# Last norm of a transformer-like layer: the scaled and shifted rows summed by TensorE in PSUM

## The chip, the cores and the metric

The kernel runs on one core of a Trainium2 chip. A core has five engines that run on their own and meet at semaphores: TensorE (PE in the profile; PEld is its weight load), VectorE (DVE), ScalarE (ACT), GpSimd (POOL), which has no access to PSUM here, and SyncE (SP), which issues the transfers that sixteen DMA engines carry out. SBUF is the working memory, PSUM the memory in which TensorE sums. The metric is the time of one execution in device microseconds, the median of several runs.

## The reference

One step of one decoder layer for 256 prompt tokens and 8x4 sample tokens, 288 tokens in all, with 2048 features. A combined input projection feeds a short gated convolution and a dilated window attention; both branches are gated, summed and projected. A layer norm follows, then a gated feed-forward net with a convolution, and the last norm:

```python
x1 = LN1(ALPHA * x + mixed @ w_out)
a, b = split(x1 @ w_up); a = causal_conv3(a)
y  = LN2(ALPHA * x1 + (silu(a) * b) @ w_down)
LN(d) = (d - mean(d)) * rsqrt(var(d) + 1e-5) * g + b       # mean and variance over the 2048 features of a token
```

All is float32. The caches are also copied to outputs. The change is in LN2 alone.

## The kernel before

Features lie on the partitions: an activation is 16 blocks of 128 features by 288 tokens. Every weight block (128 outputs by up to 16x128 inputs) is loaded from memory by SP (`prepare`, L181), cut in two parts hi and lo by ScalarE and VectorE (`split`, L230: a cast, then the remainder), in half blocks of eight 128x128 pieces with four buffers for each part, and multiplied in three terms per piece, hi x hi, hi x lo, lo x hi (`mms`, L219; lines 225, 226, 227). A product of a whole block is 48 matmuls of 288 columns, and its sum lies in one of six PSUM buffers `acc`. The same `prepare` sends, behind some loads, a copy from memory to memory of a part of the caches.

The feed-forward net runs in three parts of 16, 16 and 12 feature blocks: up products, convolution and gate, then 16 down products whose results are added to `dd`, the 16 blocks that go into LN2. In the last part each down product has 12x3 matmuls. After each of them VectorE adds the product to `dd` (L913), ScalarE squares it (L755) and GpSimd adds block and square to two sums (L760, L761); from block 1 on GpSimd has taken a rough mean `c` off the block beforehand (L910). The last block joins in TensorE: `ones_d` times the sums and the last block gives mean and mean square of each token on all partitions (L769, L770).

`finish_out` (L795) then forms the output. ScalarE squares and copies the mean (L800, L801), VectorE gets the variance (L802), ScalarE takes the reciprocal square root and its square (L808, L809), and VectorE refines it in one Newton step (L819, L820). r = 1/deviation stands in PSUM, a copy for GpSimd in SBUF (L821). Mean and r are rows by token, so they are taken off and multiplied in wide operations over 2 or 3 blocks (`by_token`, L806), on VectorE for most blocks and on GpSimd for the rest, as the lists at the top of the file say: `NORM_DVE` (L90), `MEAN_POOL`, `OUT_POOL`. The scale g and the shift b are by feature, one number per partition: ScalarE applies them in one activation per block (L830), VectorE does it for four blocks (L828). The result lies in `yah`, and six transfers, in the order of `OUT_ORDER` (L94), bring it out (L831).

The order on each engine is made by a scheduler that plans the whole program with its own estimates; `issue_after` and `behind` pin an instruction behind another. The instructions of one engine run in that order.

Of the kernel before, what the change touches and what calls it, by code (L numbers as in the profile page):

```python
# [14 lines left out]
ALU = mybir.AluOpType  # L15
# [71 lines left out]

NORM_DVE = ("m", 0, 3), ("r", 0, 3), ("m", 3, 3), ("r", 3, 3), ("m", 6, 2), ("r", 6, 2), ("r", 8, 2), ("r", 10, 2)  # L90
MEAN_POOL = (8, 2), (10, 2), (12, 2), (14, 2)
OUT_POOL = (12, 2), (14, 2)
GB_DVE = (8, 9, 10, 11)
OUT_ORDER = (0, 3), (3, 3), (6, 2), (8, 4), (12, 2), (14, 2)  # L94


@with_exitstack
def layer_kernel(ctx: ExitStack, tc: tile.TileContext, ins, outs):
# [14 lines left out]
    def sb(pl, shape, tag, dt=F32, bufs=None):  # L113
        return pl.tile(shape, dt, tag=tag, name=nm(tag), bufs=bufs)
# [10 lines left out]
    def t2(ap):  # L125

        return ap.rearrange("p (a h) -> p h a", h=2)
# [4 lines left out]
    def f32(ap):  # L132
        return ap.bitcast(F32)
# [595 lines left out]

    dd = sb(big, [P, KD, T], "dd")  # L730

    lw = sb(wk, [P, 7, T], "cache", bufs=3)

    class Norm:


        def __init__(self, g, b, tail):

            self.g, self.b, self.tail = g, b, tail
            self.s1, self.s2, self.c = (lw[:, k] for k in range(3))  # L740

        def first(self):

# [7 lines left out]
        def add(self, i):  # L751
            d = dd[:, i]
            last = i == KD - 1
            q = self.s2 if i == 0 else sb(wk, [P, T], "cy", bufs=2)
            act.activation(q, d, AF.Square)  # L755
            i_sum = None
            if i == 0:
                i_sum = pool.tensor_copy(self.s1, d)
            elif not last or not self.tail:
                pool.tensor_tensor(self.s1, self.s1, d, ALU.add)  # L760
                i_sum = pool.tensor_tensor(self.s2, self.s2, q, ALU.add)  # L761
            if i == KD - 2:

                act.activation(lw[:, 3, 0:1], q[:, 0:1], AF.Abs_reciprocal_sqrt)
            if last:
                self.p1, self.p2 = att(T), att(T)
                if self.tail:
                    for p, s, e in ((self.p1, self.s1, d), (self.p2, self.s2, q)):
                        pe.matmul(p, f32(ones_d), s, start=True, stop=False)  # L769
                        pe.matmul(p, f32(ones_d), e, start=False, stop=True)  # L770
                else:
                    w = sb(wk, [P, 4, T], "cache", F32R, bufs=3)
                    split(w[:, 0:2], w[:, 2:4], lw[:, 0:2])
# [6 lines left out]

        def finish(self):

            mu, v, r, t = (lw[:, k] for k in range(3, 7))
# [11 lines left out]
        def finish_out(self, y, out):  # L795

            mu, r_pool, t = (lw[:, k] for k in range(3, 6))
            mean, v = self.p1, self.p2
            r, dev = (sb(ps, [P, T], "acc") for _ in range(2))
            act.activation(t, mean, AF.Square)  # L800
            act.copy(mu, mean)  # L801
            i_v = dve.scalar_tensor_tensor(v, v, EPS, t, ALU.add, ALU.subtract)  # L802

            def by_token(eng, k0, n, w, op):
                k = slice(k0, k0 + n)
                return eng.tensor_tensor(dd[:, k], dd[:, k], w.unsqueeze(1).broadcast_to([P, n, T]), op)  # L806

            act.activation(r, v, AF.Abs_reciprocal_sqrt)  # L808
            act.activation(t, r, AF.Square)  # L809
            for k0, n in MEAN_POOL:  # L810
                by_token(pool, k0, n, mu, ALU.subtract)
            before = i_v
            for n_op, (what, k0, n) in enumerate(NORM_DVE):
                with tc.issue_after(before.ins):
                    before = by_token(dve, k0, n, *((mean, ALU.subtract) if what == "m" else (dev, ALU.mult)))
                if n_op == 0:

                    with tc.issue_after(before.ins):
                        dve.scalar_tensor_tensor(t, t, -0.5, v, ALU.mult, ALU.mult)  # L819
                        before = dve.scalar_tensor_tensor(dev, t, 1.5, r, ALU.add, ALU.mult)  # L820
                    act.copy(r_pool, dev)  # L821
            for k0, n in OUT_POOL:
                by_token(pool, k0, n, r_pool, ALU.mult)
            for k0, n in OUT_ORDER:
                for i in range(k0, k0 + n):
                    if i in GB_DVE:
                        with tc.issue_after(before.ins):
                            dve.tensor_scalar(t2(y[:, i]), h2(dd[:, i]), self.at(self.g, i), self.at(self.b, i), ALU.mult, ALU.add)  # L828
                    else:
                        act.activation(t2(y[:, i]), h2(dd[:, i]), AF.Identity, bias=self.at(self.b, i), scale=self.at(self.g, i))  # L830
                sp.dma_start(out[:, k0 : k0 + n, :], y[:, k0 : k0 + n, :])  # L831

# [31 lines left out]
    cf = sb(big, [P, KF, 2 + 2 * NB], "qk_s")  # L864
    f = 0
    n2 = Norm(R_LN + 2 * KD, R_LN + 3 * KD, True)
    sums = []
    for part, nf in enumerate(THIRDS):
        gh = sb(big, [P, KD, T], "yah", F32R)
        gl = sb(big, [P, KD, T], "yal", F32R)  # L870
        for k in range(nf):
            pa = product(x_gb if part == 0 else x)
            u = sb(wk, [P, UW + 2], "u", bufs=2)
            up, us = conv_in(u[:, :UW], R_SF + f * 2 * NB)
            if part == 0:
                pa, b1 = normed(pa)
                for a, b in zip(of_tokens(up, us), of_halves(pa)):
                    act.activation(a, b, AF.Identity, bias=b1)
            else:
# [12 lines left out]
            f += 1  # L892
            if part == 0:

                with tc.issue_after(i_rows.ins):
                    pool.tensor_tensor(dd[:, k], dd[:, k], n1.r, ALU.mult)
                    pool.tensor_tensor(dd[:, k], dd[:, k], n1.nmr, ALU.add)
                act.activation(dd[:, k], dd[:, k], AF.Identity, bias=n1.at(n1.b, k), scale=n1.at(n1.g, k))
        if f == KF:
            sp.dma_start(outs["o_cf"].rearrange("p (k r) -> p k r", k=KF), cf)  # L900
        for i in range(KD):
            o = product((h3(gh), h3(gl)))
            if part == 0:
                for i_x, *before in zip(split(x[0][:, i], x[1][:, i], h2(dd[:, i])), last_split, w_split):
                    for b in before:
                        behind(i_x, b)
                dve.scalar_tensor_tensor(h2(dd[:, i]), h2(dd[:, i]), ALPHA, o, ALU.mult, ALU.add)
            else:
                if f == KF and i > 0:
                    i_c = pool.tensor_tensor(dd[:, i], dd[:, i], n2.c, ALU.subtract)  # L910
                    if i > 2:
                        behind(i_c, sums[i - 3])
                dve.tensor_tensor(h2(dd[:, i]), h2(dd[:, i]), o, ALU.add)  # L913
            if f == KF:
                if i == 0:
                    n2.first()
                sums.append(n2.add(i))
    yf = sb(big, [P, KD, T], "yah")
    y_out = outs["o_y"].rearrange("p (k t) -> p k t", k=KD)
    n2.finish_out(yf, y_out)  # L920


# [181 lines left out]
```

## Time and profile before

| | |
|---|---|
| median of 3 runs | 1725.01 us (1724.82 to 1725.48) |
| the profiled execution: its own time | 1724.86 us |
| its span, first to last instruction | 1723.1 us |
| TensorE busy | 1704.4 us, 99% |
| VectorE, ScalarE, GpSimd busy | 1107.7, 870.7 and 271.1 us |
| moved by DMA | 436.16 MB, mean 253 GB/s |

A row of a timeline has the start in microseconds, the duration, the engine, the source line, the operation, what it writes `<-` what it reads with the shapes, `xN` for N merged instructions, and in brackets how long the engine was idle ahead of it and what released it. A row of the chain of waits has start, duration and the work that the end waited on. A row of a table by stretches has the stretch, its length, busy time and count of PE, PEld, DVE, ACT and POOL, the granted TensorE clock (1.00 is full), the mean busy share of the DMA engines, and GB/s. In a group of instructions the last numbers are busy microseconds, mean nanoseconds of one, and the idle time ahead of it. The rows for one line have the shortest, the median and the longest duration in nanoseconds.

### The profile page before, as it was taken

The page shows a single profiled execution, that of the slowest core. Times are in us where ns is not written, and L with a number is a line of the kernel's source. Part 1 is how long each engine was busy: PE and PEld are TensorE (multiplying, and loading weights), DVE is VectorE, ACT ScalarE, POOL GpSimd, SP SyncE. Part 2 cuts the span into 40 slices and gives each one's busy share as a digit, 9 for nine tenths or more (in the row PEclk, how much of TensorE's full clock was granted, in tenths as well). Part 3 has the DMA queues.
Part 4 walks back from the last instruction along what each step waited for, and adds up shares of the span by engine and source line. Part 5 has one row for each costly group of instructions (what it writes and reads, how often), then busy time and mean ns, then how long its engine had stood idle before and what let it go on. Part 6 is the DMA issues. An engine that isn't in the chain of part 4 may idle for free.

```text
span 1723.1 us, 33696 instructions
## 1 busy us (share of the span) xinstructions
PE 1704.4 (99%) x14096; PEld 1699.0 (99%) x14096; DVE 1107.7 (64%) x1428; ACT 870.7 (51%) x1416; POOL 271.1 (16%) x428
## 2 busy tenths in 40 slices
PE   9999999999999999999999999999999999999996
PEld 9999999999999999999999999999999999999996
DVE  6457677775777765455788888855555554555554
ACT  5446555554555554444545655544454543354444
POOL 0011110000000000011454333300111100011165
PEclk9999999999999999999999999999999999999998
DMA  8766666665667776688876666667666667767662
GB/s 294 288 258 250 237 220 252 234 242 205 262 245 253 297 285 245 245 308 302 300 264 245 246 258 254 245 251 276 255 253 261 245 250 265 268 249 261 234 233 92
DMA packets 60408, 436.16 MB, mean 253 GB/s; under 512 B 7584, under 2 KB 13472, under 8 KB 20640
## 3 DMA queue, kind: packets, MB, share of 16 engines
q1 hardware_dynamic: 58960, 430.33, 66.9%
q10 hardware_dynamic: 1296, 3.69, 0.6%
q8 instruction: 110, 1.80, 0.4%
q14 instruction: 42, 0.34, 0.1%
HBM read 427.53 MB, written 94.53 MB: 303 GB/s over the span
## 4 chain that ended last, share of the span: by engine, by line
PE 98%; DMA 0%; DVE 0%; ACT 0%; SPq 0%; ACTq 0%; issue 0%; DVEq 0%
PE acc L225 32%; PE acc L226 32%; PE acc L227 32%; PE acc L310 2%; DMA wst<-in_w_in 0%; ACT yah L830 0%; DVE dd L806 0%; PE att L513 0%; PE att L434 0%; PE att L417 0%; PE att L383 0%; PE acc L422 0%; PE att L390 0%; PE att L543 0%; PE att L430 0%; SPq L273 0%
## 5 line engine op out<-in xcount | busy, mean ns | idle before, releaser
L231 DVE TENSOR_TENSOR wlo<-wst,whi 128x1024 fp32r<-128x1024 f32 (+1 forms) x574 | 699.9, 1219 | 482.4 <-ACT whi L231 478.5
L231 ACT CAST whi<-wst 128x1024 fp32r<-128x1024 f32 (+1 forms) x574 | 586.4, 1022 | 777.7 <-PE acc L226 710.8
L225 PE MATMUL acc<-xh,whi 128*128 128x288 f32 (+1 forms) x3184 | 909.3, 286 | 0.0
L226 PE MATMUL acc<-xl,whi 128*128 128x288 f32 (+1 forms) x3184 | 907.7, 285 | 0.0
L227 PE MATMUL acc<-xh,wlo 128*128 128x288 f32 (+1 forms) x3184 | 907.6, 285 | 0.0
L225 PEld LDWEIGHTS acc<-xh,whi 128*128 128x128 f32 x3184 | 599.1, 188 | 1.4 <-issue 0.8
L227 PEld LDWEIGHTS acc<-xh,wlo 128*128 128x128 f32 x3184 | 599.1, 188 | 0.0
L226 PEld LDWEIGHTS acc<-xl,whi 128*128 128x128 f32 x3184 | 599.0, 188 | 0.0
L227 PE MATMUL acc<-yah,wlo 128*128 128x288 f32 x1216 | 347.7, 286 | 0.0
L226 PE MATMUL acc<-yal,whi 128*128 128x288 f32 x1216 | 347.7, 286 | 0.0
L225 PE MATMUL acc<-yah,whi 128*128 128x288 f32 x1216 | 347.6, 286 | 0.0
L227 PEld LDWEIGHTS acc<-yah,wlo 128*128 128x128 f32 x1216 | 229.8, 189 | 0.0
L226 PEld LDWEIGHTS acc<-yal,whi 128*128 128x128 f32 x1216 | 229.8, 189 | 0.0
L225 PEld LDWEIGHTS acc<-yah,whi 128*128 128x128 f32 x1216 | 229.7, 189 | 0.0
L667 POOL COPY qk_s<-u 128x2 f32<-128x2 f32 x44 | 37.9, 861 | 572.0 <-ACT u L881 449.1
L484 DVE TRANSPOSE_TENSOR_REDUCE sw<-cache 128x32 f32<-128x1024 f32 x64 | 79.6, 1244 | 5.2 <-ACT cache L477 1.1
L655 DVE SCALAR_TENSOR_TENSOR cy<-u,prm,cy 128x304 f32<-128x304 f32 x120 | 70.7, 589 | 3.5 <-ACT cy L653 0.7
L726 POOL TENSOR_TENSOR ya<-ya,dd 128x288 f32<-128x288 f32 x16 | 13.7, 859 | 294.4 <-DVE ya L725 288.8
L477 ACT ACTIVATE cache<-cache,qk_s 128x128 f32<-128x128 f32 x128 | 43.2, 392 | 0.0
L477 ACT ACTIVATE cache<-cache,dd 128x128 f32<-128x128 f32 x128 | 42.1, 390 | 0.0
L678 DVE TENSOR_TENSOR ya<-cy,acc 128x256 f32<-128x256 f32 x88 | 23.3, 303 | 28.1 <-PE acc L227 28.1
L231 ACT CAST yah<-ya 128x288 fp32r<-128x288 f32 x76 | 32.5, 427 | 15.7 <-DVE ya L683 8.0
(206 smaller groups left out, 972.2 us busy)
## 6 DMA issues: line engine op xcount, KB each, us to landing
wst<-in_w_in SPq DMA_DIRECT2D x111, 1024.0 KB, 4.9
wst<-in_w_up SPq DMA_DIRECT2D x88, 1024.0 KB, 4.9
wst<-in_w_down SPq DMA_DIRECT2D x32, 1024.0 KB, 4.8
cache<-in_ck SPq DMA_DIRECT2D x18, 1024.0 KB, 6.2
cache<-in_cv SPq DMA_DIRECT2D x18, 1024.0 KB, 6.1
wst<-in_w_a SPq DMA_DIRECT2D x16, 1024.0 KB, 5.0
wst<-in_w_out SPq DMA_DIRECT2D x16, 1024.0 KB, 5.0
wst<-in_w_down SPq DMA_DIRECT2D x16, 768.0 KB, 4.4
```

Of the source, the lines that this page charges most:

```text
L225: pe.matmul(out, hi[:, c, :], xh_k, start=k == 0, stop=False)
L226: pe.matmul(out, hi[:, c, :], xl_k, start=False, stop=False)
L227: last_mm[0] = pe.matmul(out, lo[:, c, :], xh_k, start=False, stop=k == nk - 1)
L231: return act.copy(hi, src), dve.tensor_tensor(lo, src, f32(hi), ALU.subtract)
L310: i = pe.matmul(o[b], first_w(term == 2, b, k, 1)[:, 0], xk, start=k == 0 and term == 0, stop=k == KD - 1 and term == 2)
L477: i = act.activation(e_t, e_t, AF.Copy, scale=w[:, g + 1, j, b * NT + t : b * NT + t + 1])
L484: dve.tensor_reduce(parts[:, g, :, j, b * NT : (b + 1) * NT].rearrange("p k j t -> p j t k"), c[:, 2 * half * cols : (2 * half + 2) * cols ...
L655: dve.scalar_tensor_tensor(y, u[:, i : i + YW], prm[:, w0 + i : w0 + i + 1], y, ALU.mult, ALU.add)
L667: pool.tensor_copy(dst[:, 0:2], u[:, SEQ : SEQ + 2])
L678: dve.tensor_tensor(a, b, c, ALU.mult)
L726: pool.tensor_tensor(m, m, ma[:, i], ALU.add)
```

## The change

The last norm is written as (g\*d - g\*mean + b\*deviation) / deviation, with deviation = v\*r. For blocks 0 to 11 a TensorE sum z in an `acc` buffer holds the bracket, and VectorE multiplies z by r in one operation per block (L874 of the changed file). Four terms may go into z:

- g\*d, as two matmuls with the identity: its hi part and its lo part. They are formed during the last down products, block by block behind the sums (`scaled`, L821; ScalarE the hi part, VectorE the rest), and lie in the tiles `xh`, `xl` of the activation x1, which nobody reads any more.
- -g\*mean, as one matmul of 65 rows: rows 0, 32 and 64 of a tile hold hi and lo of -g and hi again, against hi and lo of the mean (L837, L838).
- b\*deviation in the same way, for blocks 6 to 11 only (`N_ACT_B` = 6). Blocks 0 to 5 get b from ScalarE behind the multiplication; blocks 6 to 11 go from VectorE to the output tile.

Blocks 12 to 15 stay with GpSimd (subtraction, multiplication by r) and ScalarE (g and b), in operations of one block. The rows of g and b are brought from the parameter array by four transfers of 1024 single words, and split by ScalarE and VectorE (`rows`, L793), during the feed-forward net. The identity is copied to a tile of its own. The first five z start before mean and r are known (`AHEAD`). r now lies in SBUF, as the refinement's operand t does. The small tile `lw` of a norm is one per norm instead of one for both. Seven transfers of other sizes bring the output out.

```diff
+N_Z = 12
+AHEAD = 5
+N_ACT_B = 6
+OUT_ORDER = (0, 2), (2, 4), (6, 3), (9, 2), (11, 1), (12, 2), (14, 2)
...
+        def rows(self):
...
+                    src = ins["prm"][:, at : at + HK].rearrange("p k -> k p").unsqueeze(0)
+                    behind(sp.dma_start(t[row : row + 1], src), w_load[0])
+                    yield
+            for m in self.gb:
+                pool.memset(f32(m)[: 2 * SQ + 1], 0.0)
...
+                act.activation(hi, src, AF.Copy, scale=sign)
+                yield
+                dve.scalar_tensor_tensor(m[other : other + 1, k], src, sign, f32(hi), ALU.mult, ALU.subtract)
+                yield
+                act.activation(m[2 * SQ : 2 * SQ + 1, k], src, AF.Copy, scale=sign)
+                yield
+
+        def scaled(self, e, i):
+            if i < N_Z:
+                act.activation(e[0][:, i], h2(dd[:, i]), AF.Copy, scale=self.at(self.g, i))
+                dve.scalar_tensor_tensor(
+                    e[1][:, i], h2(dd[:, i]), self.at(self.g, i), f32(e[0][:, i]), ALU.mult, ALU.subtract
+                )
...
+            dve.scalar_tensor_tensor(v, v, EPS, t, ALU.add, ALU.subtract)
+            dve.tensor_copy(m2, mu)
+            dve.tensor_tensor(m2[low], mu[low], f32(m2[low]), ALU.subtract)
             act.activation(r, v, AF.Abs_reciprocal_sqrt)
             act.activation(t, r, AF.Square)
...
+            def z_in(i):
+                z = acc()
+                for k in range(2):
+                    row.append(pe.matmul(z, self.ident, e[k][:, i].rearrange("p h a -> p a h"), start=k == 0, stop=False))
+                return z
+
+            def z_out(n, z, i, what, stop):
+                rhs = h2(what[: 2 * SQ + 1]).rearrange("p h a -> p a h")
+                row.append(pe.matmul(z, self.gb[n][: 2 * SQ + 1, i], rhs, start=False, stop=stop))
+
+            z = [z_in(i) for i in range(AHEAD)]
+            for i in range(AHEAD):
+                z_out(0, z[i], i, m2, i < N_ACT_B)
+            for k0 in range(N_Z, KD):
+                pool.tensor_tensor(dd[:, k0], dd[:, k0], mu, ALU.subtract)
+            dve.scalar_tensor_tensor(t, t, -0.5, v, ALU.mult, ALU.mult)
+            before = dve.scalar_tensor_tensor(r, t, 1.5, r, ALU.add, ALU.mult)
+            for i in range(N_Z, KD):
+                pool.tensor_tensor(dd[:, i], dd[:, i], r, ALU.mult)
+            for i in range(N_Z):
+                if i == 2:
+                    with tc.issue_after(before.ins):
+                        before = dve.tensor_tensor(sg, v, r, ALU.mult)
+                    act.copy(s2, sg)
+                if i == 4:
+                    with tc.issue_after(before.ins):
+                        before = dve.tensor_tensor(s2[low], sg[low], f32(s2[low]), ALU.subtract)
+                    for k in range(N_ACT_B, len(z)):
+                        z_out(1, z[k], k, s2, True)
+                dst = h2(dd[:, i]) if i < N_ACT_B else t2(y[:, i])
                 with tc.issue_after(before.ins):
-                    before = by_token(dve, k0, n, *((mean, ALU.subtract) if what == "m" else (dev, ALU.mult)))
...
+                    before = dve.tensor_tensor(dst, z[i].rearrange("p a h -> p h a"), h2(r), ALU.mult)
+                if len(z) < N_Z:
+                    n = len(z)
+                    z.append(z_in(n))
+                    z_out(0, z[n], n, m2, n < N_ACT_B)
+                    if i >= 4 and n >= N_ACT_B:
+                        z_out(1, z[n], n, s2, True)
...
+                    if i < N_ACT_B:
+                        act.activation(t2(y[:, i]), h2(dd[:, i]), AF.Identity, bias=self.at(self.b, i))
+                    elif i >= N_Z:
                         act.activation(t2(y[:, i]), h2(dd[:, i]), AF.Identity, bias=self.at(self.b, i), scale=self.at(self.g, i))
                 sp.dma_start(out[:, k0 : k0 + n, :], y[:, k0 : k0 + n, :])
```

In the changed file the refinement stands at L858 and L859, the deviation and its two parts at L865, L866 and L869, the matmuls at L846 (g\*d) and L851 (the other terms), GpSimd's blocks at L857 and L861, ScalarE's output blocks at L885 and L887, and the output transfers at L888.

More of the change, by code (lines that the diff above doesn't have):

```diff
@@ L739, in __init__ @@
             self.g, self.b, self.tail = g, b, tail
-            self.s1, self.s2, self.c = (lw[:, k] for k in range(3))
+            self.lw = sb(wk, [P, 7, T], "cache", bufs=3)
+            self.s1, self.s2, self.c = (self.lw[:, k] for k in range(3))
         def first(self):
@@ L769, in add @@
                         pe.matmul(p, f32(ones_d), s, start=True, stop=False)
-                        pe.matmul(p, f32(ones_d), e, start=False, stop=True)
+                        self.last = pe.matmul(p, f32(ones_d), e, start=False, stop=True)
                 else:
                     w = sb(wk, [P, 4, T], "cache", F32R, bufs=3)
-                    split(w[:, 0:2], w[:, 2:4], lw[:, 0:2])
+                    split(w[:, 0:2], w[:, 2:4], self.lw[:, 0:2])
                     for k in range(4):
@@ L798, in finish_out @@
+        def scaled(self, e, i):
[4 more added lines that the diff above has]
+                )
+        def finish_out(self, e, y, out):
+            mu, r, t, sg = (self.lw[:, k] for k in range(3, 7))
             mean, v = self.p1, self.p2
-            r, dev = (sb(ps, [P, T], "acc") for _ in range(2))
+            m2, s2 = (sb(wk, [P, T], "h", F32R, bufs=2) for _ in range(2))
+            low = slice(2 * SQ, 3 * SQ)
@@ L822, in finish_out @@
-            for k0, n in OUT_POOL:
-                by_token(pool, k0, n, r_pool, ALU.mult)
+            row = [self.last]
+            def z_in(i):
[6 more added lines that the diff above has]
+                row.append(pe.matmul(z, self.gb[n][: 2 * SQ + 1, i], rhs, start=False, stop=stop))
@@ L824, in finish_out @@
+            in_a_row(row)
             for k0, n in OUT_ORDER:
                 for i in range(k0, k0 + n):
[L826 to L829, printed above, removed]
+                    if i < N_ACT_B:
+                        act.activation(t2(y[:, i]), h2(dd[:, i]), AF.Identity, bias=self.at(self.b, i))
+                    elif i >= N_Z:
@@ L866, in layer_kernel @@
     n2 = Norm(R_LN + 2 * KD, R_LN + 3 * KD, True)
+    rows = n2.rows()
     sums = []
@@ L892, in layer_kernel @@
             f += 1
+            if part == 1:
+                for _ in range(2):
+                    next(rows, None)
             if part == 0:
```

42 lines of the change are left out of this document (18 added, 24 removed).

## The prediction

> **What bounds the kernel now.** I read the page first (header, busy times, chain), then the chain of the last 20 us in order of time, the timelines of single engines there, and the table of busy times by stretches for the transfers.
>
> ```profile
> span 1723.1 us, 33696 instructions
> PE 1704.4 (99%) x14096; PEld 1699.0 (99%) x14096; DVE 1107.7 (64%) x1428; ACT 870.7 (51%) x1416; POOL 271.1 (16%) x428
> PE 98%; DMA 0%; DVE 0%; ACT 0%; SPq 0%; ACTq 0%; issue 0%; DVEq 0%
> ```
>
> TensorE is the bound for 1705.5 us. What the change rewrites lies behind its last product; that stretch has another limit, and is read by itself.
>
> ```profile
> 1705.49 0.12 PE acc L227
> 1706.58 0.98 PE att L770 x4
> 1707.66 0.47 DVE att L802
> 1708.13 0.95 DVE dd L806
> 1709.08 0.42 DVE cache L819
> 1709.52 0.47 DVE acc L820
> 1710.02 0.41 ACT cache L821
> 1713.59 2.75 ACT yah L830 x5
> 1716.86 1.56 ACT yah L830 x3
> ```
>
> The sums end at 1707.6, the refined 1/deviation (L820) is there at 1709.99, and ScalarE writes its last output block at 1716.86 + 1.56 = 1718.42. The span ends 4.7 us later; the transfers fill that gap.
>
> ```profile
> 1713.27 0.34 SPq L831 DMA_DIRECT2D out_o_y<-yah  x1
> 1718.45 0.33 SPq L831 DMA_DIRECT2D out_o_y<-yah  x1
> ```
> ```profile
> 1713.27:1714.00 0.73, 0.00 (x0) 0.00 (x0) 0.73 (x2) 0.41 (x1) 0.73 (x2) 0.50 0.00 0
> 1715.00:1716.00 1.00, 0.00 (x0) 0.00 (x0) 1.00 (x3) 1.00 (x3) 1.00 (x1) 0.50 0.23 86
> 1719.00:1720.00 1.00, 0.00 (x0) 0.00 (x0) 0.00 (x0) 0.00 (x0) 0.00 (x0) 0.50 1.06 424
> 1720.00:1721.00 1.00, 0.00 (x0) 0.00 (x0) 0.00 (x0) 0.00 (x0) 0.00 (x0) 0.50 0.97 380
> 1721.00:1722.00 1.00, 0.00 (x0) 0.00 (x0) 0.00 (x0) 0.00 (x0) 0.00 (x0) 0.50 0.23 85
> ```
>
> The last two columns are the DMA engines' share and GB/s. A transfer moves nothing in its first 0.73 us (I take 0.80). The engines idle around 1715.5 and are full to the end: 0.085 MB after 1721.0 at 400 GB/s (mean of 424 and 380) puts the last byte at 1721.2, 1.9 us before the span's end. One block is 128x288x4 B = 0.147 MB, 0.37 us at that rate. The last transfer alone would be done at 1718.45 + 0.80 + 2x0.37 = 1720.0, so 1.2 us of the tail is backlog: **the end is set by draining the output**, not only by computing it. The profiled execution took 1724.86 us, 1.76 over its span and 0.15 under the 1725.01 median of the runs.
>
> **The change part by part.** *Rows of g and b (L795 to L819).* Four transfers of 1024 single words each (L803), two POOL memsets, eight ScalarE and four VectorE operations over 1x1024. In the built order of the changed kernel the first two transfers stand on SP's queue behind a load and its copy, and four ScalarE operations between two weight casts, here:
>
> ```profile
> 1202.23 0.52 SPq L150 DMA_DIRECT2D out_o_rest<-in_rest  x1
> 1208.34 1.05 ACT L231 CAST whi<-wst 128x1024 fp32r<-128x1024 f32 x1 [1.56 <-PE acc L226]
> 1211.28 1.05 ACT L231 CAST whi<-wst 128x1024 fp32r<-128x1024 f32 x1 [1.89 <-PE acc L226]
> 1212.36 1.23 DVE L231 TENSOR_TENSOR wlo<-wst,whi 128x1024 fp32r<-128x1024 f32 x1 [0.50 <-ACT whi L231]
> ```
> ```profile
> out_o_rest<-in_rest SPq DMA_DIRECT2D x48, 7.1
> yal<-in_cst SPq DMA_DIRECT2D x8, 32.0 KB, 4.3
> ```
>
> Casts come every 2.94 us, one per half block. The half cast at 1211.28 has four buffers to live in, so TensorE needs it three halves later, at 1220.1; less the cast and subtraction (1.05 + 1.23, 0.2 between) its cast may start at 1217.6. Four operations at the cast's 1.05 take 4.2: the rows must have landed by 1213.4. They are issued at about 1202.8, behind a copy that lands at 1202.2 + 7.1 = 1209.3. So they have 4.1 us of their own. No row shows a transfer of single words. Bounds: nothing beyond the copy, or what a 1 MB copy itself takes, about 5 us each on the queue; the 32 KB loads (4.3 us from issue to landing, mostly waiting) are nearest by size, so I take nothing: 0. The second pair stands alike one product later. VectorE's four 1x1024 operations fit its 50% idle time there; the memsets stand before work whose input comes later.
>
> *g\*d in two parts (L821 to L826).* Twelve ScalarE and twelve VectorE operations in the last twelve-row products.
>
> ```profile
> 1693.45 0.69 DVE L231 TENSOR_TENSOR wlo<-wst,whi 128x512 fp32r<-128x512 f32 x1
> 1696.36 1.23 DVE L231 TENSOR_TENSOR wlo<-wst,whi 128x1024 fp32r<-128x1024 f32 x1 [2.22 <-ACT whi L231]
> 1693.63 0.44 ACT L755 ACTIVATE cy<-dd 128x288 f32<-128x288 f32 x1 [0.67 <-DVE dd L913]
> 1695.28 1.05 ACT L231 CAST whi<-wst 128x1024 fp32r<-128x1024 f32 x1 [1.20 <-PE acc L226]
> ```
> ```profile
> L847 ACT ACTIVATE xh<-dd,prm 128x288 fp32r<-128x288 f32 x16 | 8.5, 532 | 1.4 <-DVE dd L749 1.4
> L848 DVE SCALAR_TENSOR_TENSOR xl<-dd,prm,xh x16: 506/1051/1057, 845.8 to 929.8; 128x288 fp32r<-128x288 f32 x16
> L838 POOL TENSOR_TENSOR h<-xh,xl x16: 807/1780/1788, 827.2 to 917.0; 128x288 f32<-128x288 f32 x16
> L846 DVE TENSOR_TENSOR dd<-h,acc 128x288 f32<-128x288 f32 x15 | 6.8, 453 | 4.0 <-PE acc L227 4.0
> ```
>
> The same pair exists as L847 and L848. After the square at 1694.07, ScalarE is free until 1695.28 and takes 0.53; VectorE then takes at most 1.06, from 1694.65 to 1695.7, and is free until 1696.36. Cost 0, hidden by TensorE's products; uncovered it would be 12x1.06.
>
> *Up to 1/deviation.* L806's subtraction (0.95 on VectorE) gives way to L837 (copy, at most 0.45) and L838 (32 partitions). Without disturbance they end by 1709.03, where L819's successor starts as before, and 1/deviation stands at 1709.99: cost 0. But L838 and L859 read both inputs from SBUF, while POOL works through its subtractions; before, L819 and L820 had an operand in PSUM. The rows show the price: L848 with two SBUF inputs takes 506 ns alone and 1057 beside POOL's L838, L846 with a PSUM operand stays at 453. That is 0 to 0.55 each; L859 nearest to the long row, 0.55; L838 on a quarter of the partitions, 0.3. So r = 1709.99 + 0.85 = 1710.84. The Trainium skill ("GPSIMD Engine Reference", section Specifications) says that POOL shares its SBUF interfaces with VectorE instructions of two SBUF inputs; L846 beside L848 agrees, and by that rule both operations pay, r = 1711.1.
>
> *Outputs.* VectorE's nine wide operations and four scalings become twelve 128x288 products out of PSUM, 0.42 apart (0.45 for L846, less overlap), with L865 (0.42) and L869 (0.9, contended) between. TensorE's 42 small matmuls at 0.12 run ahead of them: blocks 0 to 4 need r anyway, blocks 9 to 11 follow L869 by 0.4 + 0.5 each. Block 8 is out at r + 10x0.42 + 0.9 = r + 5.1, block 11 at r + 6.4. ScalarE falls from twelve blocks to ten and a copy, in the built order 0, 1, copy, 12, 2, 3, 13, 4, 14, 5, 15. At 0.545 a block (2.75/5), 0.50 for those without a scale, and 0.41 for the copy, starting at r + 0.5, block 13 is out at r + 4.0, block 15 at r + 6.1.
>
> *The drain.* The built order on SP is blocks 0-1, 12-13, 6-8, 9-10, 2-5, 11, 14-15. The first leaves early. The second starts moving at r + 4.05 + 0.8 = r + 4.85 and ends at r + 5.6; 6-8 are ready only at r + 5.95, a gap of 0.35; then twelve blocks follow without one: r + 5.95 + 12x0.37 = r + 10.4. That is 1721.2 with r = 1710.84: no gain, although ScalarE is done at 1716.9 instead of 1718.42. The doubtful pieces (L838's 0.3, the gap) lean down, so I take **0.3 us off: 1724.6**. The computing saves 1.5 us, and the transfers, bunched behind it, keep nearly all.
>
> **The rivals.** *No contention:* r = 1709.99, L869 takes 0.45 instead of 0.9 and so closes the gap before 6-8: the drain ends at r + 5.6 + 4.4 = 1720.0, 1723.7 in all. Against it speaks the POOL row in this stretch:
>
> ```profile
> 1707.88 8.23 POOL L806 TENSOR_TENSOR dd<-dd,cache 128x576 f32<-128x576 f32 x6 [4.42 <-ACT cache L801]
> ```
>
> POOL will again have eight operations without a pause, 0.8 to 1.1 each.
>
> *POOL late:* at 1.1 each its sixth result, block 13, comes at 1707.9 + 6.6 = 1714.5, against ScalarE's slot at r + 3.5 = 1714.3; the second transfer waits 0.2 to 0.6, all later ones too: 1725.2.
>
> *Half clock:* with pauses between short bursts TensorE could lose its clock.
>
> ```profile
> 1711.50:1712.00 0.50, 0.00 (x0) 0.00 (x0) 0.50 (x2) 0.46 (x1) 0.50 (x2) 0.64 0.00 0
> ```
>
> The granted clock (third from the end) falls to half about 4 us after the last matmul. Blocks 9 to 11 would then come 0.98 apart, delaying 9-10 by 0.4; the drain hides half: 1724.8. The Trainium skill ("TensorE: Matmul & The Clock Gate", Part 1) gives an idle window of about 3.4 us; the row agrees, and bursts during r to r + 3 may hold it off.
>
> *Slower, the rows come late:* one mechanism, ScalarE held at L814. It decides from a landing at 1213.4, and then costs a microsecond for each. With 5 us for each of the two transfers, 1219.3: 5.9 us, 1730.5. For it: 1024 pieces against 128 in a 1 MB load; the Trainium skill ("DMA: Bandwidth & Descriptors", Rules for kernel authors) says that a strided last dimension becomes one descriptor per element, which no run here shows yet. Against it: 4 KB in all.
>
> **How the numbers follow.** Forecast 0.50; no contention 0.24; POOL late or half clock 0.15; rows late 0.11. A measurement of this kernel can tell about 0.2% (3.45 us) from no change. The tail cannot give that: sixteen blocks at 0.37 behind a first issue at r + 1.6, with r = 1709.99, end at 1718.3 at best, 2.9 earlier. So faster 0.02, within 0.89, slower 0.09 (most of the late rows). Range 1723.2 (no contention, 0.5 less for shorter operations) to 1727.0 (POOL late and the first 2 us of late rows).
>
> **What would show it.** The last output activation near 1716.9; L859 at about 1.0 us and L838 above 0.5; DMA share near 1 from 6-8's start to the end, with the last byte at 1720.9; no idle TensorE near 1215 to 1230. Wrong if TensorE waits there, if L859 stays at 0.46, or if the transfers pause between 1716 and 1720.

## The result and the profile after

| | before | after |
|---|---|---|
| median of 6 runs | 1724.85 us (1724.6 to 1725.48) | 1739.4 us (1738.0 to 1740.09) |
| ratio to before, 95% interval | | 1.0083 (1.007 to 1.0096) |
| the profiled execution, its span | 1724.86, 1723.1 us | 1739.72, 1737.9 us |

The changed kernel is 0.8% slower, 14.6 us. The page of the changed kernel, header, small packets and the chain that ended last by engine:

```profile
span 1737.9 us, 33825 instructions
...
DMA packets 64681, 436.18 MB, mean 251 GB/s; under 512 B 11728, under 2 KB 17744, under 8 KB 24912
...
PE 96%; DMA 2%; ACT 1%; DVE 0%; issue 0%; SPq 0%; ACTq 0%; DVEq 0%
```

TensorE's share of the chain fell from 98% to 96%, and transfers, which had 0%, now hold 2%. To split the loss at the end of the last product, take VectorE's operation that adds that product to `dd` (L913 before). The timeline of VectorE in the changed kernel, at that operation and up to 1/deviation:

```profile
1720.98 0.45 DVE L974 TENSOR_TENSOR dd<-dd,acc 128x288 f32<-128x288 f32 x1 [3.96 <-PE acc L226]
...
1723.31 0.80 DVE L837 CAST h<-cache 128x288 fp32r<-128x288 f32 x1
1724.14 0.93 DVE L838 TENSOR_TENSOR h<-cache,h 32x288 fp32r<-32x288 f32 x1
...
1725.59 0.46 DVE L859 SCALAR_TENSOR_TENSOR cache<-cache 128x288 f32<-128x288 f32 x1
```

In the kernel before the last addition starts at 1705.71:

```profile
1705.71 0.46 DVE L913 TENSOR_TENSOR dd<-dd,acc 128x288 f32<-128x288 f32 x1 [3.96 <-PE acc L227]
```

So the products end 1720.98 - 1705.71 = 15.27 us later, while the tail from there to the end of the span shrank from 1723.1 - 1705.71 = 17.39 to 1737.9 - 1720.98 = 16.92 us, by 0.47. The whole loss lies in front of the part that was rewritten. Where it is, the timelines of TensorE, of ScalarE and of SP's queue show. TensorE, the matmuls that had to wait:

```profile
1223.38 0.39 PE L224 MATMUL acc<-xh,whi 128*128 128x288 f32 x1 [2.86 <-ACT whi L230]
1224.64 0.61 PE L226 MATMUL acc<-xh,wlo 128*128 128x288 f32 x1 [0.75 <-DVE wlo L230]
...
1244.75 0.61 PE L224 MATMUL acc<-xh,whi 128*128 128x288 f32 x1 [6.69 <-ACT whi L230]
1246.01 0.61 PE L226 MATMUL acc<-xh,wlo 128*128 128x288 f32 x1 [0.41 <-DVE wlo L230]
```

ScalarE around the operations on the rows (L814 is the first of each pair):

```profile
1208.66 1.05 ACT L230 CAST whi<-wst 128x1024 fp32r<-128x1024 f32 x1 [1.56 <-PE acc L225]
1217.96 1.06 ACT L814 ACTIVATE cache<-ybh 1x1024 fp32r<-1x1024 f32 x1 [8.24 <-DMA ybh<-in_prm]
...
1222.28 2.94 ACT L230 CAST whi<-wst 128x1024 fp32r<-128x1024 f32 x3
...
1239.34 1.06 ACT L814 ACTIVATE cache<-ybl 1x1024 fp32r<-1x1024 f32 x1 [10.97 <-DMA ybl<-in_prm]
```

SP's queue (a row of two transfers spans both issues and what SP waits between them):

```profile
1203.16 6.11 SPq L803 DMA_DIRECT2D ybh<-in_prm  x2
1209.36 15.57 SPq L185 DMA_DIRECT2D wst<-in_w_up  x2
...
1225.62 6.49 SPq L803 DMA_DIRECT2D ybl<-in_prm  x2
```

And all issues of the row transfers, with the shortest, the median and the longest duration of an issue in nanoseconds:

```profile
L803 SPq DMA_DIRECT2D ybh<-in_prm x2: 821/3025/5229, 1203.2 to 1204.0; - x2
L803 SPq DMA_DIRECT2D ybl<-in_prm x2: 715/3222/5729, 1225.6 to 1226.4; - x2
```

The first pair of rows is issued from 1203.16 on. ScalarE's first operation at L814 reads the row of g, which the first of the two transfers brings; it is released at 1217.9, 14.7 us after that issue. The first issue of the pair takes 0.8 us; the second holds SP for 5.2 us. ScalarE stands at L814 for 8.24 us, its next weight casts come at 1222.28, and TensorE has run out of weights. The second pair repeats it with 10.97 us, and TensorE then idles 6.69 + 0.41. The waits sum to 10.7 us; most of what remains of the 15.27 is told by the table by stretches, whose third column from the end is the granted clock:

```profile
1224.00:1225.00 1.00, 0.36 (x1) 0.37 (x2) 1.00 (x2) 1.00 (x2) 0.00 (x0) 0.80 0.00 0
...
1227.00:1228.00 1.00, 1.00 (x6) 1.00 (x6) 0.96 (x3) 0.22 (x2) 0.00 (x0) 0.50 0.94 377
1228.00:1229.00 1.00, 1.00 (x10) 1.00 (x10) 1.00 (x1) 0.36 (x1) 0.98 (x2) 1.00 2.38 918
1241.00:1242.00 1.00, 0.00 (x0) 0.00 (x0) 0.64 (x1) 0.98 (x2) 0.00 (x0) 0.83 0.28 115
...
1248.00:1249.00 1.00, 1.00 (x8) 1.00 (x7) 1.00 (x2) 0.90 (x1) 0.65 (x1) 0.76 0.96 401
```

The clock is at half for a time after each gap. A share of 0.80 means that 0.4 us of that microsecond were at half, so the clock is low from 1224.6 to 1228.0, and again from 1241.7 to 1248.5. Undisturbed matmuls start 0.123 us apart; summing what successive starts lie further apart than that gives 5.8 us around the first gap (3.9 at the waits, 1.8 at the half clock) and 9.2 around the second (7.6 and 1.6). With 0.33 us by which this execution was already late before the rows were asked for (its copy is issued at 1202.56, before at 1202.23), this is 15.3, against 15.27 measured.

### The profile page after: what moved, and what is told of

Its sections match the earlier page's. It is cut to its first block, busy times and chain, and to the rows that moved or that the text cites. A ratio compares the mean times of both kernels' runs of the same rounds, so it can differ in the third digit from the quotient of the medians.

```text
span 1737.9 us, 33825 instructions
## 1 busy us (share of the span) xinstructions
PE 1716.1 (99%) x14138; PEld 1709.4 (98%) x14138; DVE 1124.2 (65%) x1448; ACT 884.0 (51%) x1435; POOL 276.2 (16%) x432
## 2 busy tenths in 40 slices
DMA packets 64681, 436.18 MB, mean 251 GB/s; under 512 B 11728, under 2 KB 17744, under 8 KB 24912
## 4 chain that ended last, share of the span: by engine, by line
PE 96%; DMA 2%; ACT 1%; DVE 0%; issue 0%; SPq 0%; ACTq 0%; DVEq 0%
PE acc L224 31%; PE acc L225 31%; PE acc L226 31%; PE acc L309 2%; DMA ybh<-in_prm 1%; DMA ybl<-in_prm 1%; DMA wst<-in_w_in 0%; ACT cache L814 0%; PE att L512 0%; DVE wlo L230 0%; PE att L433 0%; ACT cache L818 0%; ACT whi L230 0%; ACT yah L885 0%; PE att L416 0%; PE att L382 0%
## 5 line engine op out<-in xcount | busy, mean ns | idle before, releaser
L654 DVE SCALAR_TENSOR_TENSOR cy<-u,prm,cy 128x304 f32<-128x304 f32 x120 | 75.9, 633 | 3.7 <-ACT cy L652 0.7
```

The lines of the kernel that those rows point to most:

```text
L654: dve.scalar_tensor_tensor(y, u[:, i : i + YW], prm[:, w0 + i : w0 + i + 1], y, ALU.mult, ALU.add)
```

## The experiments

Line numbers of the experiments' kernels differ by a few from those of the changed kernel. The kernel before, run beside them, had medians of 1725.08, 1725.31 and 1724.98 us in the three batches.

**The rows from contiguous memory.** The same rows out of an added input, one run of 4 KB for each transfer instead of 1024 single words.

```diff
-src = ins["prm"][:, at : at + HK].rearrange("p k -> k p").unsqueeze(0)
+src = ins["lnr"][row // SQ : row // SQ + 1, half * HK * P : (half + 1) * HK * P].rearrange("o (k p) -> o k p", p=P)
...
+"lnr": np.stack([a["ln2_g"], a["ln2_b"]]),
```

> The changed kernel with one difference: the rows of g and b of the last norm lie ready as two contiguous rows in an input array, so that each of the four transfers moves 4 KB in one run instead of 1024 single words. Same places on all queues, same operations. Theory (the transfers of single words are the whole loss): the rows land in time, TensorE is never idle between 1215 and 1250 us, and what is left is the tail, 0.47 us shorter than before: 1724.4. Rival (the eight ScalarE and four VectorE operations on the rows, 4.2 us in a row between two casts, hold the casts): idle TensorE remains, 1728 or more. Rival (the g*d parts in the last products delay something): time remains behind 1300 us, 1725 to 1727.

1725.07 us (1724.18 to 1725.36, 11 runs), ratio 0.9999 (0.999 to 1.0008), span 1722.6. The last addition, the wait for the second pair, SP's queue and the packets of this kernel:

```profile
1705.67 0.46 DVE L973 TENSOR_TENSOR dd<-dd,acc 128x288 f32<-128x288 f32 x1 [3.95 <-PE acc L226]
```
```profile
1223.58 1.06 ACT L813 ACTIVATE cache<-ybl 1x1024 fp32r<-1x1024 f32 x1 [2.12 <-DMA ybl<-in_lnr]
```
```profile
1202.80 1.00 SPq L802 DMA_DIRECT2D ybh<-in_lnr  x2
1207.69 8.56 SPq L185 DMA_DIRECT2D wst<-in_w_up  x2
...
1216.87 0.94 SPq L802 DMA_DIRECT2D ybl<-in_lnr  x2
```
```profile
DMA packets 60561, 436.18 MB, mean 253 GB/s; under 512 B 7604, under 2 KB 13620, under 8 KB 20792
```

The last addition is back at 1705.67, and TensorE waits for no weights. Only how four transfers read memory was altered, so the whole 15 us hang on that. The time that was expected, 1724.4, didn't come: the tail is as short as in the changed kernel in the profiled execution (16.93 us), but the medians of this kernel and of the one before are the same, and the interval of the ratio is wider than half a microsecond. The packets under 512 B differ by 11728 - 7604 = 4124, close to the 4 x 1024 = 4096 words. The Trainium skill ("DMA: Bandwidth & Descriptors", Rules for kernel authors) has a strided last dimension become one descriptor per element; this count agrees.

**The transfers without a reader.** The kernel before with the four transfers of words at the same places, and nobody who reads what they bring.

```diff
+for row, c in ((0, n2.g), (SQ, n2.b)):
+    at = c + half * HK
+    src = ins["prm"][:, at : at + HK].rearrange("p k -> k p").unsqueeze(0)
+    behind(sp.dma_start(t[row : row + 1], src), w_load[0])
...
+if part == 1:
+    for _ in range(2):
+        next(rows, None)
```

> The kernel before with the four transfers of 1024 single words added at the same places of SP's queue, and nobody reads them. It tells the wait for the rows from what the transfers do to the queue and to the loads behind them. Theory A (ScalarE held at the first operation on the rows is the loss): 1725 to 1726, no idle TensorE. Theory B (the loads of weights behind the transfers come late, whoever waits): several us of idle TensorE, 1728 to 1738.

1725.79 us (one run), span 1724.0. SP's queue and VectorE's last addition:

```profile
1203.25 0.52 SPq L150 DMA_DIRECT2D out_o_rest<-in_rest  x1
1203.86 6.20 SPq L874 DMA_DIRECT2D ybh<-in_prm  x2
...
1215.64 10.13 SPq L874 DMA_DIRECT2D ybl<-in_prm  x2
```
```profile
1706.73 0.46 DVE L927 TENSOR_TENSOR dd<-dd,acc 128x288 f32<-128x288 f32 x1 [3.96 <-PE acc L227]
```

SP is held as long by the first pair, 6.20 us, and longer by the second, 10.13 us from 1215.64 on. The weight loads behind them start late, but TensorE doesn't wait for them. The execution is 1.02 us late both before the transfers (1203.25 against 1202.23) and at the last addition (1706.73 against 1705.71): between these two points the transfers cost nothing. So neither their traffic nor the late loads make the loss by themselves; it takes ScalarE's wait.

**What a transfer of words takes.** The kernel before with four transfers of 2 or 4 KB in the quiet second part, each read by a copy on GpSimd: A, 1024 words gathered into one partition (the form of the change); B, 1024 words to 128 partitions; C, 4 KB as one run; D, 512 words that lie together in memory, put into every second word of one partition.

```diff
+if n == 0: d, src = t[0:1], ins["prm"][:, n2.g : n2.g + HK].rearrange("p k -> k p").unsqueeze(0)
+elif n == 1: d, src = t[:, 0, 0:HK], ins["prm"][:, n2.g : n2.g + KD : 2]
+elif n == 2: d, src = t[0:1].rearrange("o k p -> o (k p)"), ins["prm"][0:1, 0 : HK * P]
+else: d, src = t[0:1].rearrange("o k p -> o (k p)")[:, 0 : HK * P : 2], ins["prm"][0:1, 0 : HK * P // 2]
+behind(sp.dma_start(d, src), w_load[0])
+pool.tensor_copy(u, u)
```

> The kernel before with four small transfers set apart in the down products of the second part, each read by one GpSimd copy that shows when it landed: (A) 1024 single words from 128 memory rows into one partition, as in the change; (B) 1024 single words over 128 partitions, eight each; (C) 4 KB in one run into one partition; (D) 512 single words from one contiguous run into every second word of one partition. If the count of pieces costs, A and B take long alike and D half. If the one partition costs, A takes long, D half of it, B little. If the scattered source costs, A and B are long, D short. C lands within 5 us in all cases. Each holds the load behind it; TensorE has some 6 us to spare, so 1725 to 1728.

1725.19 us (one run). The issues of A, B and C on SP's queue, and the copies on GpSimd that wait for them:

```profile
1385.37 0.83 SPq L878 DMA_DIRECT2D ybh<-in_prm  x1
1409.47 0.58 SPq L878 DMA_DIRECT2D ybl<-in_prm  x1
1433.22 0.39 SPq L878 DMA_DIRECT2D ybh<-in_prm  x1
```
```profile
1394.36 0.18 POOL L880 COPY ybh<-ybh 1x8 f32<-1x8 f32 x1 [7.99 <-DMA ybh<-in_prm]
1416.38 0.99 POOL L880 COPY ybl<-ybl 128x8 f32<-128x8 f32 x1 [18.24 <-DMA ybl<-in_prm]
1439.43 0.18 POOL L880 COPY ybh<-ybh 1x8 f32<-1x8 f32 x1 [22.06 <-DMA ybh<-in_prm]
```

From issue to use A takes 9.0 us, B 6.9, C 6.2, and D 6.8 (1455.94 to 1462.75). C was expected within 5 us. The four don't stand alike on the queue: ahead of A and D there is a weight load, ahead of B and C a load and a copy. Of like place, B takes 0.7 more than C, and A 2.2 more than D. A takes 2.8 more than C, although C has the copy ahead of it, so the form of the change adds at least that for 4 KB. The weight load ahead of A lands late as well: 8.5 us after its issue, against 6.3 ahead of D and 4.8 ahead of B and of C.

B brings as many words from as many rows of memory, so the count of pieces alone isn't it, nor the scattered source. What remains is the one partition, which D shares with half of the words, and the number of DMA engines that share the work. The semaphore signals in the trace tell of the latter: after the issue the landing of A is signalled eight times (1393.69 to 1394.24), of B and D sixteen times, of C once. If each engine signals once for its share, the form of the change ran on eight of the sixteen engines. No run tries the same words on all sixteen, so the two aren't separated.

A pair takes longer than these probes say: the first of its transfers lands 14.7 us after its issue, A 9.0. By the DMA packets in the trace the last single word of the first pair is done at 1213.2; the landing of the first transfer is signalled at 1217.9, that of the second at 1218.9. What holds the first signal for 4.7 us, and what holds SP at the second issue, was not tried; a single transfer of words, here and in the next experiment, issues in 0.8 us.

**The words early, their use late.** The changed kernel with the transfers of words one at a time and the operations on the rows held back into the third part.

```diff
-for _ in range(2):
+if part == 1 and k < 5 or part == 2:
+    late[0] = last_split[0] if part == 2 else None
+    for _ in range(1 if part == 1 else 3):
         next(rows, None)
...
+if late[0] is not None:
+    behind(i_hi, late[0])
```

> The changed kernel with the four transfers one at a time, each about 12 us apart or more in the second part, and the operations on the rows in the third part, some hundreds of us later. If the loss is the wait for rows that have not landed, it goes: 1724.4 to 1725. If a transfer of single words also makes the loads behind it late by more than the buffers carry, idle TensorE remains at each of the four: 1726 to 1735.

1724.77 us (one run), span 1723.0. No engine waits for the rows, and the last addition starts at 1705.82, 0.11 behind that of the kernel before. The words need no other layout if they have time.

**The first pair alone.** The changed kernel with the first pair fetched word by word, and the second as 4 KB runs.

```diff
+if half == 0:
+    src = ins["prm"][:, at : at + HK].rearrange("p k -> k p").unsqueeze(0)
+else:
+    src = ins["lnr"][row // SQ : row // SQ + 1, half * HK * P : (half + 1) * HK * P].rearrange("o (k p) -> o k p", p=P)
```

> The changed kernel with only the first pair of rows fetched word by word; the second pair comes from the contiguous array as 4 KB runs. It prices the first late landing alone. Theory (each late pair holds ScalarE, and the second costs more than the first because TensorE then runs right behind the casts): ScalarE waits about 8 us for the first pair, TensorE idles 2.9 + 0.75 = 3.6 us, then runs about 2 us of work at half clock; the second pair lands soon enough that TensorE doesn't idle again for more than 1 us. Last product ends 5 to 7 us behind that of the kernel before, time about 1730 to 1732. Rival (the loss is mostly one event, the queue being blocked by the first pair, and the second pair only inherits it): TensorE idles again by 5 us or more, time about 1738.

1732.55 us (one run), span 1730.7, between what the two theories gave. The waiting matmuls, ScalarE's wait for the second pair, SP's queue and the clock:

```profile
1222.79 0.39 PE L224 MATMUL acc<-xh,whi 128*128 128x288 f32 x1 [1.61 <-ACT whi L230]
1224.05 0.39 PE L226 MATMUL acc<-xh,wlo 128*128 128x288 f32 x1 [0.75 <-DVE wlo L230]
...
1237.12 0.39 PE L224 MATMUL acc<-xh,whi 128*128 128x288 f32 x1 [1.27 <-ACT whi L230]
1238.38 0.39 PE L226 MATMUL acc<-xh,wlo 128*128 128x288 f32 x1 [0.75 <-DVE wlo L230]
```
```profile
1231.70 1.06 ACT L817 ACTIVATE cache<-ybl 1x1024 fp32r<-1x1024 f32 x1 [3.92 <-DMA ybl<-in_lnr]
```
```profile
1210.13 14.23 SPq L185 DMA_DIRECT2D wst<-in_w_up  x2
...
1225.04 0.82 SPq L806 DMA_DIRECT2D ybl<-in_lnr  x2
```
```profile
1239.00:1240.00 1.00, 1.00 (x9) 1.00 (x8) 1.00 (x2) 0.91 (x4) 0.35 (x2) 0.74 0.51 74
1240.00:1241.00 1.00, 1.00 (x6) 1.00 (x6) 1.00 (x2) 1.00 (x2) 1.00 (x1) 0.50 0.86 360
...
1242.00:1243.00 1.00, 1.00 (x7) 1.00 (x6) 1.00 (x1) 0.66 (x2) 0.88 (x2) 0.56 2.92 1245
```

By the starts of matmuls the first gap costs 2.9 us and keeps the clock. The second pair, fast now, still costs 2.6 at its gap and 1.7 at half clock. With the 1.0 us by which this execution was late before (its copy is issued at 1203.22) that is 8.1 before rounding, as much as the last addition is late (1713.82 against 1705.71). The second pair lands 6.7 us after its issue (at 1231.7), as in the kernel with runs alone (1216.87 to 1223.58), where it harmed nothing. What differs is the issue: 8.2 us later, while TensorE is only 2.9 + 1.0 us later. The queue says why: ahead of that issue stands a weight load held for most of 14.23 us, 8.56 with runs alone. SP's longest wait for VectorE to free a weight buffer, the last number of each row, in the changed kernel and in the kernel before:

```profile
SPq L185 <- DVE wlo L230: 1344.5, 280, 13.5
```
```profile
SPq L186 <- DVE wlo L231: 1330.2, 278, 7.4
```

That buffer is freed by the split of a weight block whose cast stands behind the first pair's operations on ScalarE. So the first wait makes the second: ScalarE held, no buffer freed, the load and the second pair behind it issued late, ScalarE held again. For the changed kernel the sum closes, with one term fitted from this experiment: the second issue is 1225.62 - 1216.87 = 8.75 us late, the words take 13.7 us instead of 6.7, TensorE is 0.33 + 5.8 us late itself, and in this experiment a landing later by 8.2 - 3.9 = 4.3 us against TensorE gave a gap of 1.27, so 3.0 were to spare: 8.75 + 7.0 - 6.1 - 3.0 = 6.6, and the gap is 6.69.

**The tail: contention and the order of outputs.** Three more kernels start from the one with runs, and a fourth from the one with the late use. The first leaves GpSimd's four subtractions of the mean out (blocks 12 to 15 aren't centred):

```diff
-for k0 in range(N_Z, KD):
-    pool.tensor_tensor(dd[:, k0], dd[:, k0], mu, ALU.subtract)
```

> The kernel with contiguous rows, without GpSimd's four subtractions of the mean (left out, so blocks 12 to 15 of the output are not centred). Contention: VectorE's copy falls from 0.80 to about 0.4 and its subtraction over 32 partitions from 0.93 to about 0.45, while the refinement (0.46) stays. No contention: both stay.

The second takes the parts of the mean out of PSUM, the hi part on ScalarE:

```diff
-dve.tensor_copy(m2, mu)
-dve.tensor_tensor(m2[low], mu[low], f32(m2[low]), ALU.subtract)
+act.copy(m2, mean)
+dve.tensor_tensor(m2[low], mean[low], f32(m2[low]), ALU.subtract)
```

> The kernel with contiguous rows, and the two parts of the mean taken from PSUM: ScalarE copies the hi part (one copy more), VectorE subtracts it from the mean in PSUM; VectorE's copy goes. Theory (VectorE's copy and subtraction are slow, 0.80 and 0.93 us, because both inputs lie in SBUF beside GpSimd's subtractions): the subtraction takes about 0.45, 1/deviation stands 0.7 to 0.9 us earlier after the end of the sums, and the last byte of the output leaves as much earlier. Rival (32 partitions or the rounding type make them slow): the subtraction stays near 0.9.

The third adds a finer order of outputs to the second, and was run twice:

```diff
-OUT_ORDER = (0, 2), (2, 4), (6, 3), (9, 2), (11, 1), (12, 2), (14, 2)
+OUT_ORDER = (0, 2), (2, 2), (4, 2), (6, 3), (9, 2), (11, 1), (12, 2), (14, 2)
```

> As the kernel with contiguous rows and the mean's parts from PSUM, and the output of blocks 2 to 5 leaves in two transfers of two blocks instead of one of four. If the tail is set by draining the output from the second transfer on, that transfer is issued 0.5 us earlier after 1/deviation and the drain ends as much earlier: together 1.5 to 2.0 us off the kernel before, 1723.0 to 1723.6, ratio 0.999. If ScalarE's last block sets the end: 0.8 us off at most.

> The kernel of e8_out_order again, to narrow its interval. If its tail is really about 1.3 us shorter: ratio 0.9990 to 0.9995, 1723.5 to 1724.2. If the first measurement was luck: 0.9997 or more.

The fourth needs no added input: the transfers of words spread out and used late, with the edits of the second and the third.

> No new input array: the word transfers spread out and used late as in e4_late_use, the subtraction for the low part out of PSUM as in e6_mean_act and the finer order of outputs of e8_out_order. Theory: transfers hidden, tail as in e8_out_order, so 1723.8 against 1725.1 before (ratio 0.9990 to 0.9996). Rival (word transfers cost something even when nobody waits): 1724.5 or more, ratio 1.000.

| kernel | us | ratio, interval | tail from the last addition |
|---|---|---|---|
| before | 1724.85 | | 17.39 |
| changed | 1739.4 | 1.0083 (1.007 to 1.0096) | 16.92 |
| rows as runs | 1725.07 | 0.9999 (0.999 to 1.0008) | 16.93 |
| without GpSimd's subtractions | 1725.41 (one run) | | 16.95 |
| mean from PSUM | 1724.48 (one run) | | 16.65 |
| and the finer order | 1723.77 (11 runs) | 0.9992 (0.9983 to 1.0001) | 16.09 |
| the same again | 1723.96 (11 runs) | 0.9994 (0.9985 to 1.0003) | 16.19 |
| words late, with both edits | 1723.75 (11 runs) | 0.9992 (0.9983 to 1.0001) | 16.18 |

VectorE's timeline without the subtractions, the copy, the difference and the end of the refinement:

```profile
1708.97 0.30 DVE L836 CAST h<-cache 128x288 fp32r<-128x288 f32 x1
1709.31 0.45 DVE L837 TENSOR_TENSOR h<-cache,h 32x288 fp32r<-32x288 f32 x1
...
1710.50 0.46 DVE L856 SCALAR_TENSOR_TENSOR cache<-cache 128x288 f32<-128x288 f32 x1
```

The same with the mean from PSUM:

```profile
1708.50 0.46 DVE L837 TENSOR_TENSOR h<-att,h 32x288 fp32r<-32x288 f32 x1
...
1709.91 0.92 DVE L858 SCALAR_TENSOR_TENSOR cache<-cache 128x288 f32<-128x288 f32 x1
```

Without GpSimd beside them the copy takes 0.30 instead of 0.80 and the difference 0.45 instead of 0.93, and 1/deviation stands 4.31 us after the last addition starts (4.27 before the change, 5.07 with it). So contention made the whole of the delay. But the tail is no shorter for it, 16.95, which the expectation doesn't speak of: the difference for b now waits 0.44 us for ScalarE's copy and then takes 1.00 us beside GpSimd's multiplications (0.45 with the rows as runs alone), and the clock is at half from 1714.1 on; VectorE's last product ends 7.98 us after 1/deviation, against 6.0 with the rows as runs alone. With the mean from PSUM the difference takes 0.46, and the end of the refinement, 0.46 in the changed kernel, takes 0.92: the disturbance moved, and of the 0.7 to 0.9 us expected 1/deviation gains 0.29. The finer order brings 0.5 to 0.6 more. The three measurements of it lie 1.0 to 1.5 us under the kernel before, like the tail (1.2 to 1.3). That is between the two expectations, 1.5 to 2.0 if the drain sets the end and 0.8 at most if ScalarE's last block does. Each interval still reaches 1.000: a gain of 0.06 to 0.08% that these runs don't show for certain.

## Why the prediction was wrong

- **Rows of g and b**, the step that failed (the landing of the rows at ScalarE): "No row shows a transfer of single words" and then "I take nothing: 0". What it cost was 14.9 us, 15.27 less the 0.33 from ahead of it. The rows were to land with the copy, at 1209.3, 6.5 us after their issue. Fetched as 4 KB runs they do take about that, 6.7; as words the first row took 14.7 and landed at 1217.9, 4.5 us behind the prediction's own limit of 1213.4. The nearest row was chosen by size, a 32 KB load; that load moves 32 runs of 1 KB, so by its form the transfer had no near row. The bound named beside it, 5 us each, with a landing at 1219.3, was the better figure. That it came so close is partly luck: the two transfers don't follow each other at 5 us, the second landed 1.0 us behind the first. The prediction's own sign of being wrong, TensorE waiting between 1215 and 1230, is what came.
- **The rival of the late rows** had the mechanism and the place: ScalarE held at L814. Its point of decision fits too: 4.5 us late by its rule, 3.9 us of lost matmul time at the first gap. Its 5.9 us was too low by two terms. The clock, at half after each gap, took 3.4 us; the prediction used it for the tail alone. And "The second pair stands alike one product later" missed that this pair's issue stands behind a load that waits for a cast that stands behind the first pair: 7.6 us at the second gap. The 3.9, 3.4 and 7.6 make the 14.9.
- **SP's queue**: the issue of the second transfer of a pair was not costed at all. It holds SP for 5.2 and 5.7 us. This costs nothing by itself, as the unread transfers show; whether it makes the landing later was not tried.
- **g\*d in two parts**, cost 0: right as far as these runs tell. With the rows as runs the last addition starts at 1705.67 against 1705.71, so 24 operations more beside the last products cost TensorE nothing there. It is one execution of each; in the other kernels without late rows that addition starts between 1705.2 and 1706.7.
- **Up to 1/deviation**, +0.85 us: measured 5.07 - 4.27 = 0.80. The sum came out by luck, its parts didn't: L859, priced at 0.55 more, stayed at 0.46, another of the prediction's signs of being wrong; L838 took 0.48 more where 0.3 was priced; and L837, priced without contention, took 0.80 instead of 0.30. The Trainium skill ("GPSIMD Engine Reference", Specifications) names two kinds of VectorE instructions that contend with GpSimd, those with two SBUF inputs and those in a mode that uses two ports; the prediction used the first kind alone. Of its two operations with two SBUF inputs one paid here, and the copy, with one input, paid as well. Up to 1/deviation none did without GpSimd's subtractions.
- **Outputs and drain**: 1/deviation plus 10.4 us predicted for the last byte. Measured 10.05, from the last stretch of the changed kernel's table in which bytes move:

```profile
1736.00:1737.00 1.00, 0.00 (x0) 0.00 (x0) 0.00 (x0) 0.00 (x0) 0.00 (x0) 0.50 0.09 32
```

  At 400 GB/s those 0.032 MB end at 1736.1; 1/deviation stands at 1726.05. L869, priced at 0.9, took 0.45, and the gap of 0.35 us ahead of blocks 6 to 8 didn't come: from 1731 to 1736 the share of the DMA engines is 0.94 or more. The tail gained 0.47 us in the profiled execution, predicted was 0.3. The finer order, which shortens the tail by half a microsecond with the same arithmetic, supports that the drain sets the end.
- **The rivals of the tail**: without GpSimd's subtractions 1/deviation stands where the rival of no contention has it, 4.31 us after the last addition starts (4.28 by the prediction), but the end didn't come earlier. Half clock didn't come in the profiled execution of the changed kernel before 1733, but came at 1711.5 with the rows as runs, and the tails are the same, 16.92 and 16.93. With the mean from PSUM it came at 1712.6, and there the last three products on VectorE start 0.96 us apart, as that rival had it (0.98).

## What to carry to other kernels

Look at a transfer's pieces before its bytes: 4 KB as single words into one partition took at least 2.8 us more than as one run, and the first of two such transfers in a row took 14.7 us to land. A small side transfer belongs where nobody who feeds the bounding engine waits for it: give it another layout, or a use much later, as the kernels at 1725.07 and 1724.77 us did. When a side task sits in the order of an engine that feeds the bound, follow what its wait holds back on other queues: here it delayed a load, the load the next side transfer, and the second gap was larger than the first.

## What the runs showed of the hardware that was not expected

The granted clock changes on a fixed grid. In the changed kernel it is low from 1224.6 to 1228.0 (3.4 us) and from 1241.7 to 1248.5 (6.8), and full for 13.7 us between; in the experiment with the first pair alone it is low for 3.4 us from 1239.5. All are multiples of 3.4, and the next fall, at 1733.2 in the changed kernel, lies 484.7 us behind 1248.5, which is 142 steps of 3.413. The Trainium skill ("TensorE: Matmul & The Clock Gate", Part 1) gives a free-running window of 3413 ns, and the trace agrees. The idle window that the prediction takes from there need not be idle throughout: on the same grid the stretch 1236.1 to 1239.5 of that experiment held 11 of the 28 matmuls that fit and was followed by half clock, the stretches 1219.0 to 1222.4 and 1222.4 to 1225.8, across the first gap, held 16 each and were not. The limit lies somewhere between, so whether waits of 2 us or so cost the clock hangs on where they fall in the grid: within one execution 1.27 + 0.75 us of waiting did, and 1.61 + 0.75 did not.

The other surprise is that an operation on VectorE with a single SBUF input, the copy L837, is slowed by GpSimd too, from 0.30 to 0.80 us, while one with two inputs a little later (L859) is not. The same end of the refinement took 0.92 with the mean from PSUM. What picks the disturbed operation stays open, and no run here shows whether the copy ran in a mode with two ports.
